# The first 30 microseconds and the last 8 of a decoder trunk: turning the input ahead of all weights, splitting the first weight in two halves, and a shorter final norm

## The chip, the cores and the metric

One Trainium2 chip, one of its cores. The metric is the device time of one execution in microseconds, the median of the runs shown; less is better.

## The reference, cut to what matters

```python
def rmsnorm(x, g):
    y = x * lax.rsqrt(jnp.mean(x * x, axis=-1, keepdims=True) + EPS)
    return y * g

def swiglu(h, w_gate, w_up, w_down):
    return (jax.nn.silu(h @ w_gate) * (h @ w_up)) @ w_down

for i in range(2):                       # x: 512 tokens x 1024
    x = x + 0.5 * swiglu(rmsnorm(x, ffn1_norm[i]), ffn1_w_gate[i], ffn1_w_up[i], ffn1_w_down[i])
    x = x + mixer[i](rmsnorm(x, mix_norm[i]))      # 0: gated linear attention, 1: stick-breaking attention
    x = x + 0.5 * swiglu(rmsnorm(x, ffn2_norm[i]), ffn2_w_gate[i], ffn2_w_up[i], ffn2_w_down[i])
return rmsnorm(x, final_norm)
```

All is float32; the feed-forward width is 2816.

## The kernel before, in words

The residual x is kept turned, as eight tiles `xs[k]` of 128 features x 512 tokens. Every product is made of three TensorE products in float32r (`mm3`, and `prod` in `seven`): each operand is cut into a high part (a cast on ACT, ScalarE) and a low part (a subtraction on DVE, VectorE), and high x high, low x high and high x low are summed. So each weight that arrives costs a cast on ACT (`wh`, L124) and a subtraction on DVE (`wl`, L126).

Weights pass through a queue, `feed`. An `Entry` is a piece of weight with its product; `feed.start()` cuts the weights of the next entries, issues their loads on SP's queue some entries ahead, and returns a generator whose steps are the products. `feat` makes one column block: 128 features x 512 tokens, 8 steps over the 1024 inputs, 24 TensorE products, in `ps_f`. The first two column blocks of the first feed-forward layer have weights of their own of 128 columns (`lead`, four loads of 512 KB: gate, up, gate, up), the next ones 256 columns. From the third 256 columns on, `seven` makes seven products of half size from sums of the weight and of the input (Strassen's form with 7 in place of 8), in two entries: `body_1` and `body_2`, in `ps_w`, `ps_q`, `ps_z`.

A layer starts before its norm is known: gains are multiplied into x ahead, the products run on that, and the norm's factor R is multiplied in when a product is taken out of its bank (`t`, L645 and L652). R comes from the row sums of squares (`stats_a`, with `rstd`: scale and add, square root on ACT, reciprocal on DVE, one Newton step, `r`), and from four products `ps_R` that spread r over the partitions (`stats_b`, which builds the diagonal tiles `dg` and copies `R` out of the bank, L405). `two_halves` starts two entries and runs them in turns, with `stats_a` in between. After the first six column blocks, the input is used with its norm already in (`scaled`: `xn`; cut into `nh`, `nl`), and `seven` also needs sums of it (`ts`, cut into `th`, `tl`).

The start of the program (L1228 to L1280): the gains are loaded into one tile `gl` by four loads on ACT's queue, turned by one TensorE product and copied to `gT`. x is loaded in eight tiles of 128 tokens x 512 features, four of the first half of the features, then the first gate weight, then the other four, then the three other first weights. Each `ps_x` bank takes four turned blocks; from it ACT makes the scaled high part (`xh`, L1260), DVE the low part (`xl`, L1261), and one of both the copy `xs[k]` (L1269, L1271). The squares of the untouched tiles of x (`junk`, L1278) run on ACT, with the row sums as a by-product.

Each engine runs its own instructions in the order in which the built program has them. A scheduler makes this order from the program text, by priorities and by what is ready; `tc.issue_after(ins)` sets an instruction behind another in it. Memory that is used again is waited for.

The last layer (`last`): the down product is made token by token block (`back_tok`), for each of four token blocks two halves of the features. `last` adds the residual on DVE, takes squares on ACT with their sum, and after the second half computes r for the block (`rstd` with n=1), scales both halves by r and the final gain (`fin`), and writes both out.

## Time and profile before

| | |
|---|---|
| Median of 3 runs | 1874.41 us (1874.35 to 1876.14) |
| Profiled execution | 1874.33 us, span from first to last instruction 1872.2 us |
| TensorE (PE) busy | 1847.3 us, 99% of the span |
| VectorE (DVE) busy | 1412.0 us, 75% |
| ScalarE (ACT) busy | 1012.5 us, 54% |
| Granted TensorE clock, mean | 0.998 of full speed |
| DMA, mean | 96 GB/s; 158 in the first fortieth of the span |

A row of the timeline has the start in us, the duration of one (or of so many, xN), the engine, the line of the source, the operation, what it writes and reads (buffer numbers left out), and in brackets how long the engine was idle just before and what ended that. PE is TensorE's product, PEld its weight load. A row of the list of waits has the engine and tile that waited, on what, then us in total, times, and the longest. A row of the table by stretches has the length, then for each engine busy us and instructions, the granted clock, the DMA engines' busy share, and GB/s. An engine's operations overlap a little: durations are longer than the distance from start to start.

### The profile page before, as it was taken

The numbers are of one execution on the slowest core, as the hardware profiler recorded it, in microseconds if no ns is written. First come the engines' busy times: TensorE is split into PE (matmuls) and PEld (weight loads), VectorE is DVE, ScalarE is ACT, GpSimd is POOL, SyncE is SP. The second block draws the span as 40 slices with busy tenths as digits, with TensorE's granted clock in tenths as the row PEclk, the third lists the DMA queues.
The fourth block names the chain that finished last, engine by engine and source line by source line (L and its number), as shares of the span: only waits on it lengthen the run. The fifth ranks groups of instructions, "written<-read, shape, count | busy, mean of one in ns | idle before, by whom it ended". The sixth has DMA issues, their size and how long they took to land.

```text
span 1872.2 us, 29140 instructions
## 1 busy us (share of the span) xinstructions
PE 1847.3 (99%) x11933; PEld 1650.8 (88%) x11933; DVE 1412.0 (75%) x2177; ACT 1012.5 (54%) x1714; POOL 7.3 (0%) x17
## 2 busy tenths in 40 slices
PE   8999999999999999999999999999999999999998
PEld 6899999789888899999888999998888788999997
DVE  7977776775767987777788777676878769777775
ACT  6544545444555554454555545445878755554454
POOL 0000000100000000000000000000000000000000
PEclk9999999999999999999999999999999999999999
DMA  5433333212123233342233333233221223333321
GB/s 158 130 107 110 105 113 103 87 48 66 61 75 113 79 102 102 107 129 80 79 113 116 111 102 113 79 92 101 68 68 57 68 90 113 102 102 102 119 85 68
DMA packets 177513, 179.04 MB, mean 96 GB/s; under 512 B 4034, under 2 KB 167924, under 8 KB 177380
## 3 DMA queue, kind: packets, MB, share of 16 engines
q1 hardware_dynamic: 176768, 176.18, 30.0%
q8 instruction: 93, 1.52, 0.3%
q0 software_dynamic: 512, 0.99, 0.2%
q14 instruction: 40, 0.33, 0.1%
q10 hardware_dynamic: 100, 0.03, 0.0%
HBM read 175.11 MB, written 2.10 MB: 95 GB/s over the span
## 4 chain that ended last, share of the span: by engine, by line
PE 88%; DVE 9%; ACT 1%; issue 1%; DMA 0%; SPq 0%; DVEq 0%; ACTq 0%
PE ps_d L64 25%; PE ps_w L523 20%; PE ps_f L64 11%; PE ps_q L523 10%; PE ps_z L523 5%; PE ps_t L64 5%; PE ps_b L64 4%; DVE wl L126 2%; PE ps_S L64 1%; PE ps_z L1058 1%; PE ps_bt L64 1%; DVE ts L615 1%; DVE xn L599 1%; DVE nl L606 1%; PE ps_oT L1120 1%; PE ps_T L1105 1%
## 5 line engine op out<-in xcount | busy, mean ns | idle before, releaser
L126 DVE TENSOR_TENSOR wl<-raw,wh 128x1024 fp32r<-128x1024 f32 x244 | 259.9, 1066 | 96.6 <-ACT wh L124 61.5
L124 ACT CAST wh<-raw 128x1024 fp32r<-128x1024 f32 x244 | 224.7, 923 | 131.2 <-PE ps_f L64 44.4
L64 PE MATMUL ps_d<-hh,wl 128*128 128x512 f32 x672 | 262.4, 390 | 0.0
L64 PE MATMUL ps_d<-hh,wh 128*128 128x512 f32 x672 | 262.3, 390 | 0.0
L64 PE MATMUL ps_d<-hl,wh 128*128 128x512 f32 x672 | 261.6, 389 | 0.0
L523 PE MATMUL ps_w<-th,wl 128*128 128x256 f32 x864 | 239.1, 277 | 5.0 <-DVE wl L126 5.0
L523 PE MATMUL ps_w<-tl,wh 128*128 128x256 f32 x864 | 239.0, 277 | 0.9 <-DVE tl L606 0.9
L523 PE MATMUL ps_w<-th,wh 128*128 128x256 f32 x864 | 239.2, 277 | 0.2
L307 DVE SCALAR_TENSOR_TENSOR x<-ps_d,x 128x512 f32<-128x512 f32 x184 | 124.9, 689 | 115.9 <-PE ps_d L64 115.6
L126 DVE TENSOR_TENSOR wl<-s,wh 128x1024 fp32r<-128x1024 f32 x144 | 176.1, 1223 | 40.7 <-PE ps_z L523 19.3
L124 ACT CAST wh<-s 128x1024 fp32r<-128x1024 f32 x144 | 151.2, 1050 | 93.2 <-PE ps_q L523 30.0
L124 ACT CAST wh<-rawd 128x1024 fp32r<-128x1024 f32 x84 | 88.4, 1053 | 201.7 <-issue 98.9
L64 PE MATMUL ps_f<-xh,wh 128*128 128x512 f32 x448 | 182.1, 407 | 1.6 <-DVE q L721 1.5
L64 PE MATMUL ps_f<-xl,wh 128*128 128x512 f32 x448 | 175.5, 392 | 0.0
L64 PE MATMUL ps_f<-xh,wl 128*128 128x512 f32 x448 | 175.0, 391 | 0.0
L523 PEld LDWEIGHTS ps_w<-th,wl 128*128 128x128 f32 x864 | 162.3, 188 | 5.8 <-DVE wl L126 5.8
L523 PEld LDWEIGHTS ps_w<-tl,wh 128*128 128x128 f32 x864 | 162.2, 188 | 1.1 <-DVE tl L606 1.1
L523 PEld LDWEIGHTS ps_w<-th,wh 128*128 128x128 f32 x864 | 162.2, 188 | 1.0 <-ACT wh L124 1.0
L64 PEld LDWEIGHTS ps_d<-hl,wh 128*128 128x128 f32 x672 | 126.2, 188 | 26.7
L64 PEld LDWEIGHTS ps_d<-hh,wh 128*128 128x128 f32 x672 | 126.2, 188 | 24.5
L64 PEld LDWEIGHTS ps_d<-hh,wl 128*128 128x128 f32 x672 | 126.2, 188 | 23.8
L126 DVE TENSOR_TENSOR wl<-rawd,wh 128x1024 fp32r<-128x1024 f32 x84 | 102.9, 1225 | 53.6 <-ACT wh L124 40.1
(248 smaller groups left out, 4434.4 us busy)
## 6 DMA issues: line engine op xcount, KB each, us to landing
raw<-in_ffn_w_gate_dram SPq DMA_DIRECT2D x43, 1024.0 KB, 5.3
raw<-in_ffn_w_up_dram SPq DMA_DIRECT2D x43, 1024.0 KB, 5.4
rawd<-in_ffn_w_down_dram SPq DMA_DIRECT2D x84, 512.0 KB, 3.5
raw<-in_gla_w_in_dram SPq DMA_DIRECT2D x12, 1024.0 KB, 5.5
raw<-in_sb_w_in_dram SPq DMA_DIRECT2D x16, 512.0 KB, 3.8
raw<-in_gla_w_out_dram SPq DMA_DIRECT2D x4, 1024.0 KB, 5.0
raw<-in_sb_w_in_dram SPq DMA_DIRECT2D x4, 1024.0 KB, 5.3
raw<-in_sb_w_out_dram SPq DMA_DIRECT2D x4, 1024.0 KB, 5.0
```

Source lines behind the costliest of these rows:

```text
L64: st["pe"] = nc.tensor.matmul(ps, l, r, start=first, stop=last).ins
L124: st["cut"] = nc.scalar.copy(h, r).ins
L126: nc.vector.tensor_tensor(out=l, in0=r, in1=h.bitcast(F32), op=ALU.subtract)
L307: nc.vector.scalar_tensor_tensor(out=xs[k], in0=ps, scalar=0.5, in1=xs[k], op0=ALU.mult, op1=ALU.add)
L523: st["pe"] = nc.tensor.matmul(o, l_, r_, start=first and j + n == 0, stop=j == 3 and n == 2, skip_group_check=True).ins
L599: nc.vector.scalar_tensor_tensor(out=t, in0=xs[k], scalar=g, in1=st["R"], op0=ALU.mult, op1=ALU.mult)
L606: nc.vector.tensor_tensor(out=l, in0=t, in1=h.bitcast(F32), op=ALU.subtract)
L615: nc.vector.tensor_tensor(out=o, in0=p, in1=q, op=ALU.subtract)
L1058: nc.tensor.matmul(o_, l_, r_, start=first, stop=last, skip_group_check=True)
L1105: nc.tensor.transpose(ps[:, c0 : c0 + P], ys[yb][:, yc + j * P : yc + (j + 1) * P], ident)
L1120: nc.tensor.matmul(po[e * 64 : e * 64 + 64, j * P : T], self.v[j][:, c : c + 64], self.wt[p, e][bk][:, c0 : c0 + n], start=j == 0, stop=j ...
```

## The change

- x is loaded whole ahead of all weights; the first gate weight comes behind it in two loads of four of its eight k-blocks each (`parts`), and is cut in two halves too.
- The gains are split over two tiles, so that those of the first norm need one load only; the rest is turned later.
- x is turned tile by tile (four blocks per tile into four banks at once) instead of bank by bank; three more banks follow for the second half, and the eighth later.
- The order of scalings, copies and cuts on ACT and DVE is set by hand (`behind`); six of the eight squares stand behind the cut of the third weight. The constraint that held the cuts behind the gains goes.
- The first column block is started by hand in the start of the program; the first `two_halves` then starts one entry instead of two.
- In `rstd` the sum isn't divided by D: D x EPS is added, and the square root of D goes into the constants of the Newton step. With n=1, two of its multiplications become one, and the sum of the two halves' squares goes into the first addition.
- In `last` the scaled first half is written to a tile of its own (`xf`) instead of over x.

```diff
@@ Chunk.load @@
-                nc.sync.dma_start(self.t, self.src)
+                for c in range(self.parts):
+                    c = slice(c * self.n // self.parts, (c + 1) * self.n // self.parts)
+                    nc.sync.dma_start(self.t[:, c], self.src[:, c])
@@ Entry.split @@
-                    st["cut"] = nc.scalar.copy(h, r).ins
-                    with tc.issue_after(st["gains"]):
-                        nc.vector.tensor_tensor(out=l, in0=r, in1=h.bitcast(F32), op=ALU.subtract)
+                    self.cut = []
+                    for c in range(parts):
+                        c = slice(c * n // parts, (c + 1) * n // parts)
+                        st["cut"] = (
+                            nc.scalar.copy(h[:, c], r[:, c]).ins,
+                            nc.vector.tensor_tensor(
+                                out=l[:, c], in0=r[:, c], in1=h[:, c].bitcast(F32), op=ALU.subtract
+                            ).ins,
+                        )
+                        self.cut.append(st["cut"])
@@ rstd @@
-    def rstd(sums, n):
+    def rstd(sums, n, more=None):
...
-        nc.vector.tensor_scalar(out=v, in0=sums, scalar1=1.0 / D, scalar2=EPS, op0=ALU.mult, op1=ALU.add)
+        nc.vector.tensor_scalar(
+            out=v, in0=sums, scalar1=0.0 if more is None else more, scalar2=D * EPS, op0=ALU.add, op1=ALU.add
+        )
...
-        nc.vector.tensor_tensor(out=q, in0=y, in1=y, op=ALU.mult)
-        nc.vector.tensor_tensor(out=q, in0=q, in1=v, op=ALU.mult)
-        nc.vector.tensor_scalar(out=q, in0=q, scalar1=-0.5, scalar2=1.5, op0=ALU.mult, op1=ALU.add)
+        if n == 1:
+            nc.vector.scalar_tensor_tensor(out=q, in0=y, scalar=v, in1=y, op0=ALU.mult, op1=ALU.mult)
+        else:
+            nc.vector.tensor_tensor(out=q, in0=y, in1=y, op=ALU.mult)
+            nc.vector.tensor_tensor(out=q, in0=q, in1=v, op=ALU.mult)
+        c = float(D) ** 0.5
+        nc.vector.tensor_scalar(out=q, in0=q, scalar1=-0.5 * c, scalar2=1.5 * c, op0=ALU.mult, op1=ALU.add)
@@ two_halves @@
-    def two_halves(between=None):
+    def two_halves(between=None, n=2):
...
-        g = [feed.start(), feed.start()]
+        g = [feed.start() for _ in range(n)]
@@ FFN.run @@
-                two_halves(stats_a)
+                two_halves(stats_a, 2 - (feed.pos == 1))
@@ last @@
         if dh == 0:
-            nc.vector.tensor_tensor(out=x, in0=x, in1=fin[:, 0:T], op=ALU.mult)
+            st["xf"] = st["tp"].tile([P, T], F32, tag="s", bufs=4, name="xf")
+            nc.vector.tensor_tensor(out=st["xf"], in0=x, in1=fin[:, 0:T], op=ALU.mult)
             return
-        s = st["sq"][:, 2 * i : 2 * i + 1]
-        nc.vector.tensor_tensor(out=s, in0=s, in1=sq, op=ALU.add)
-        r = rstd(s, 1)
+        r = rstd(sq, 1, st["sq"][:, 2 * i : 2 * i + 1])
...
-        nc.scalar.activation(xt[i, 0], xt[i, 0], AF.Copy, scale=r)
-        nc.sync.dma_start(rows[:, 0:T], xt[i, 0])
+        nc.scalar.activation(st["xf"], st["xf"], AF.Copy, scale=r)
+        nc.sync.dma_start(rows[:, 0:T], st["xf"])
```

The start of the program is written anew. Its order after the change:

```python
for hf in range(2):
    for i in range(NT):
        x0[i, hf] = ip.tile([P, T], F32, name=f"x0_{i}_{hf}")
        nc.sync.dma_start(x0[i, hf], a["x"][0, i * P : (i + 1) * P, hf * T : (hf + 1) * T])
for c in lead:
    c.pool, c.parts = ip, 2 if c is lead[0] else 1
    c.load()
...
squares(0, (0, 1))
pst = [psum("ps_x") for _ in range(4)]
for i in range(NT):
    if i == 2:
        ...                                     # gains of the first norm: turn, copy
    for k in range(4):
        turn(k, pst[k], i)
done = [scale(k, pst[k]) for k in range(4)]     # xh on ACT, xl on DVE
kept = [keep(k, pst[k]) for k in range(2)]      # xs[k]: even k on ACT, odd k on DVE
pst += [psum("ps_x") for _ in range(3)]
with tc.issue_after(st["pe"]):
    for i in range(NT):
        for k in range(4, 7):
            turn(k, pst[k], i)
with behind([kept[0], kept[1]]):
    feed.q[0].split(parts=2)
pst.append(psum("ps_x"))
...                                             # turn k = 7
with behind(feed.q[0].cut[0]):
    done += [scale(k, pst[k]) for k in range(4, 8)]
    kept += [keep(k, pst[k]) for k in range(2, 4)]
with tc.issue_after(st["pe"]):
    body = feed.q[0].body(feed.q[0].W)
    next(body)                                  # first half of the first column block
with behind(done[7]):
    feed.q[1].split()
    with behind(st["cut"]):
        kept += [keep(k, pst[k]) for k in range(4, 8)]
for _ in body:
    pass
with behind(kept[6:]):
    feed.start()
...                                             # the other gains: turn, copy
with behind(st["cut"]):
    squares(0, (2, 3))
    squares(1, range(NT))
```

More of the change, by code (lines that the diff above doesn't have):

```diff
@@ L79, in __init__ @@
             self.few = False
+            self.parts = 1
         def load(self):
@@ L105, in view, with split @@
             return self.views
-        def split(self):
+        def split(self, parts=1):
             if self.W is None:
@@ L1183, in to_tokens @@
     def to_tokens(tp):
+        st["tp"] = tp
         fin = st["fin"] = tp.tile([P, D], F32, tag="s", bufs=4, name="fin")
@@ L1228, in decoder, with gains @@
     with tc.tile_pool(name="ip", bufs=1) as ip:
-        gl = ip.tile([P, P], F32, name="gl")
-        nc.vector.memset(gl, 0.0)
-        row = 0
-        for nm in ("ffn1_norm", "mix_norm", "ffn2_norm"):
-            nc.scalar.dma_start(gl[row : row + 16], a[nm].rearrange("l (k p) -> (l k) p", p=P))
-            row += 16
-        nc.scalar.dma_start(gl[row : row + 2], a["gla_o_norm"].rearrange("l (k p) -> (l k) p", p=P))
+        gls = [ip.tile([P, P], F32, name=f"gl{n}") for n in range(2)]
+        for gl in gls:
+            nc.vector.memset(gl, 0.0)
+        def gains(n, names):
+            row = n * 16
+            for nm in names:
+                r = a[nm].rearrange("l (k p) -> (l k) p", p=P)
+                nc.scalar.dma_start(gls[n][row : row + r.shape[0]], r)
+                row += r.shape[0]
+        gains(0, ("ffn1_norm",))
+        gains(1, ("mix_norm", "ffn2_norm", "gla_o_norm"))
         x0 = {}
-        st["ss"] = None
-        sums = [ip.tile([P, NT], F32, name=f"sums{hf}") for hf in range(2)]
-        lead = phases[0].lead
         for hf in range(2):
@@ L1243, in decoder @@
                 nc.sync.dma_start(x0[i, hf], a["x"][0, i * P : (i + 1) * P, hf * T : (hf + 1) * T])
-            for c in lead[:1] if hf == 0 else lead[1:]:
-                c.pool = ip
-                c.load()
-        ps = psum("ps_g")
-        nc.tensor.transpose(ps[:, 0:P], gl, ident)
-        st["gains"] = nc.vector.tensor_copy(gT[:, 0:50], ps[:, 0:50]).ins
-        st["nh"], st["nl"], pst = [], [], []
-        for hf in range(2):
-            for k in range(hf * 4, hf * 4 + 4):
-                ps = psum("ps_x")
-                for i in range(NT):
-                    nc.tensor.transpose(
-                        ps[:, i * P : (i + 1) * P], x0[i, hf][:, (k % 4) * P : (k % 4 + 1) * P], ident
-                    )
-                h = np_.tile([P, T], F32R, tag="xh", name="xh")
-                l = np_.tile([P, T], F32R, tag="xl", name="xl")
-                nc.scalar.activation(h, ps, AF.Copy, scale=gT[:, k : k + 1])
-                nc.vector.scalar_tensor_tensor(
-                    out=l, in0=ps, scalar=gT[:, k : k + 1], in1=h.bitcast(F32), op0=ALU.mult, op1=ALU.subtract
-                )
-                st["nh"].append(h)
-                st["nl"].append(l)
-                pst.append(ps)
-            for k in range(hf * 4, hf * 4 + 4):
-                if k % 2:
-                    nc.vector.tensor_copy(xs[k], pst[k])
-                else:
-                    nc.scalar.copy(xs[k], pst[k])
@@ L1272, in decoder @@
-        for e in feed.q[:2]:
-            e.split()
-        for hf in range(2):
-            for i in range(NT):
-                junk = ip.tile([P, T], F32, tag="j", bufs=2, name="junk")
-                with tc.issue_after(st["cut"]) if hf * NT + i >= 6 else ExitStack():
-                    nc.scalar.activation(junk, x0[i, hf], AF.Square, accum_out=sums[hf][:, i : i + 1])
+        lead = phases[0].lead
+        for c in lead:
+            c.pool, c.parts = ip, 2 if c is lead[0] else 1
+            c.load()
@@ new lines, in decoder, with squares, behind @@
+        st["ss"] = None
+        sums = [ip.tile([P, NT], F32, name=f"sums{hf}") for hf in range(2)]
+        st["nh"], st["nl"] = [], []
+        new_norm()
+        def squares(hf, tiles):
+            for i in tiles:
+                junk = ip.tile([P, T], F32, tag="j", bufs=2, name="junk")
+                nc.scalar.activation(junk, x0[i, hf], AF.Square, accum_out=sums[hf][:, i : i + 1])
+        def behind(ins):
+            es = ExitStack()
+            for c in ins:
+                es.enter_context(tc.issue_after(c))
+            return es
@@ new lines, in turn, with scale @@
+        def turn(k, ps, i):
+            x = x0[i, k // 4]
+            t = nc.tensor.transpose(ps[:, i * P : (i + 1) * P], x[:, (k % 4) * P : (k % 4 + 1) * P], ident)
+            st["pe"] = t.ins
+        def scale(k, ps):
+            h = np_.tile([P, T], F32R, tag="xh", name="xh")
+            l = np_.tile([P, T], F32R, tag="xl", name="xl")
+            c = nc.scalar.activation(h, ps, AF.Copy, scale=gT[:, k : k + 1]).ins
+            d = nc.vector.scalar_tensor_tensor(
+                out=l, in0=ps, scalar=gT[:, k : k + 1], in1=h.bitcast(F32), op0=ALU.mult, op1=ALU.subtract
+            ).ins
+            st["nh"].append(h)
+            st["nl"].append(l)
+            return c, d
@@ new lines, in keep @@
+        def keep(k, ps):
+            if k % 2:
+                return nc.vector.tensor_copy(xs[k], ps).ins
+            return nc.scalar.copy(xs[k], ps).ins
+        squares(0, (0, 1))
+        pst = [psum("ps_x") for _ in range(4)]
+        for i in range(NT):
+            if i == 2:
+                psg = psum("ps_g")
+                nc.tensor.transpose(psg[:, 0:P], gls[0], ident)
+                nc.vector.tensor_copy(gT[:, 0:16], psg[:, 0:16])
+            for k in range(4):
+                turn(k, pst[k], i)
@@ new lines, in decoder @@
+        done = [scale(k, pst[k]) for k in range(4)]
+        kept = [keep(k, pst[k]) for k in range(2)]
+        pst += [psum("ps_x") for _ in range(3)]
+        with tc.issue_after(st["pe"]):
+            for i in range(NT):
+                for k in range(4, 7):
[4 more added lines that the diff above has]
+        with tc.issue_after(st["pe"]):
+            for i in range(NT):
+                turn(7, pst[7], i)
@@ new lines, in decoder @@
+        with behind(feed.q[0].cut[0]):
+            done += [scale(k, pst[k]) for k in range(4, 8)]
+            kept += [keep(k, pst[k]) for k in range(2, 4)]
+        with tc.issue_after(st["pe"]):
+            body = feed.q[0].body(feed.q[0].W)
[5 more added lines that the diff above has]
+        for _ in body:
+            pass
+        with behind(kept[6:]):
+            feed.start()
@@ L1279, in decoder @@
+        ps = psum("ps_g")
+        with tc.issue_after(st["pe"]):
+            nc.tensor.transpose(ps[:, 0:P], gls[1], ident)
+        nc.vector.tensor_copy(gT[:, 16:50], ps[:, 16:50])
+        with behind(st["cut"]):
+            squares(0, (2, 3))
+            squares(1, range(NT))
         st["sums"] = sp.tile([P, NT], F32, tag="rq", bufs=2, name="sums")
```

## The prediction

> **What bounds the kernel now.** I read the page's chain first, then the list of waits of TensorE (whole span, then its first 80 us), then busy time by stretches of 5 us, and last the timeline of the first 70 us and of the last 8.

> ```profile
> PE 88%; DVE 9%; ACT 1%; issue 1%; DMA 0%; SPq 0%; DVEq 0%; ACTq 0%
> PE ps_g L1248 <- DMA gl<-in_ffn_norm_dram: 5.8, 1, 5.8
> PE ps_w L523 <- DVE wl L126: 1.4, 1, 1.4
> core 0: us, PE busy (x) PEld busy (x) DVE busy (x) ACT busy (x) POOL busy (x), PEclk, DMA share, GB/s
> 0.00:5.00 5.00, 0.00 (x0) 0.00 (x0) 0.22 (x2) 1.96 (x4) 0.70 (x6) 1.00 0.54 174
> 5.00:10.00 5.00, 3.98 (x17) 3.35 (x17) 0.23 (x2) 3.09 (x8) 0.00 (x0) 1.00 0.91 269
> 10.00:15.00 5.00, 3.65 (x18) 2.99 (x19) 3.90 (x6) 4.49 (x10) 0.00 (x0) 0.81 1.16 326
> 30.00:35.00 5.00, 5.00 (x24) 4.14 (x23) 5.00 (x10) 3.44 (x5) 0.00 (x0) 1.00 0.01 3
> 60.00:65.00 5.00, 5.00 (x44) 4.92 (x43) 5.00 (x9) 2.00 (x6) 0.00 (x0) 1.00 0.00 0
> 65.00:70.00 5.00, 3.58 (x28) 3.19 (x27) 5.00 (x7) 3.76 (x7) 0.00 (x0) 1.00 0.70 210
> ```

> TensorE carries 88% of the chain; only its wait for the first gains (5.8 us, hidden by the loads of x) and one of 1.4 us for VectorE (DVE) stand out in the first 80 us. But DVE's 9% matters here: from 30 to 70 us it is busy all of every stretch. The 1.4 us wait lies at the end of this full stretch. So two clocks run through the start: TensorE, and DVE's unbroken queue from the moment when R (the row norm, spread over the partitions) exists. Whichever is later sets everything behind 70 us, where TensorE doesn't wait up to 200 us and the built order of TensorE is the same before and after.

> ```profile
> 6.76 2.63 PEld L1255 LDWEIGHTS ps_x<-ident,x 128*128 128x128 f32 x13 [0.26 <-DMA x<-in_x_dram]
> 12.34 2.35 PE L1255 MATMUL ps_x<-ident,x 128*128 128x128 f32 x13 [0.41 <-DMA x<-in_x_dram]
> 14.34 0.78 PE L64 MATMUL ps_f<-xh,wh 128*128 128x512 f32 x1
> 16.80 0.39 PE L64 MATMUL ps_f<-xh,wh 128*128 128x512 f32 x1
> 18.62 0.39 PE L64 MATMUL ps_f<-xl,wh 128*128 128x512 f32 x1
> 26.03 0.16 DVE L388 TENSOR_TENSOR r<-ry,rq 128x4 f32<-128x4 f32 x1
> 26.77 1.09 PE L401 MATMUL ps_R<-dg,gT 128*128 128x128 f32 x8
> 28.51 1.22 DVE L126 TENSOR_TENSOR wl<-raw,wh 128x1024 fp32r<-128x1024 f32 x1
> 29.64 0.69 DVE L645 TENSOR_TENSOR t<-ps_f,R 128x512 f32<-128x512 f32 x1
> 66.02 0.38 PE L523 MATMUL ps_w<-th,wh 128*128 128x256 f32 x1
> 66.50 1.23 DVE L126 TENSOR_TENSOR wl<-s,wh 128x1024 fp32r<-128x1024 f32 x1
> 67.78 0.38 PE L523 MATMUL ps_w<-th,wl 128*128 128x256 f32 x1 [1.37 <-DVE wl L126]
> 69.18 0.28 PE L523 MATMUL ps_q<-nh,wh 128*128 128x256 f32 x1
> 69.37 1.23 DVE L126 TENSOR_TENSOR wl<-raw,wh 128x1024 fp32r<-128x1024 f32 x1
> ```

> Landmarks: the fourth tile of x is there by 6.76, the last at 12.34; products begin at 14.34 and run at (18.62-16.80)/8 = 0.2275 us; r is computed at 26.03, and I call tR the time at which DVE first multiplies by R, 29.64. The first product of body_2 then waits for DVE until 67.78, and the next (ps_q) begins at 69.18, which is tR + 39.54. TensorE alone would have been 1.4 us earlier.

> **The change at the front: TensorE starts sooner.** All eight tiles of x now pass before the weights on SP's queue. Two bounds for the second half of the first gate weight (2.1 + 0.52 = 2.62 MB lie up to its end): by the stretches, 0.87 + 1.345 MB have moved by 10.0, and the other 0.41 MB take 1.24 us at 326 GB/s, so 11.2; and in the trace the transfer with the same 2.62 MB up to its end is the last tile of x, 12.34. I take 12.34, the same bytes in the same queue with like transfers behind it, and keep 11.2 for the range. The first half, 0.26 MB ahead at 326 GB/s, lands 0.8 earlier, 11.5. The transposes, gains (now from one load) and the first four scalings are done by then: from 7.4 (fourth tile at 6.76, its turn behind the third's four, 0.2 each) four scalings of 0.61 and one copy of 0.6 (rows below) give 10.4. Products begin near 12.3, 2.0 us earlier than 14.34. Keeping copies (L1269, L1271) behind other work, the second memset and the second turn of gains (0.2 us each) fall into idle time of DVE and cost nothing; without that cover they would add their 0.2.

> **The change to R: it comes later.** The squares of six tiles, which ran in ACT's gaps while it waited for loads, now stand in ACT's order behind three weight casts, and the fourth cast and the table load stand behind the squares. ACT's order in the built program from the second half cast on: four scalings, x2, the up cast, x4, x6, a gate cast, six squares, an up cast, table load, square root.

> ```profile
> 13.57 2.43 ACT L1260 ACTIVATE xh<-ps_x,gT 128x512 fp32r<-128x512 f32 x4
> 17.47 0.64 ACT L1271 COPY x<-ps_x 128x512 f32<-128x512 f32 x1
> 17.93 1.12 ACT L124 CAST wh<-raw 128x1024 fp32r<-128x1024 f32 x1
> 19.97 0.71 ACT L1278 ACTIVATE junk<-x 128x512 f32<-128x512 f32 x1
> 20.60 3.01 ACT L124 CAST wh<-raw 128x1024 fp32r<-128x1024 f32 x3
> 23.62 1.28 ACT L381 ACT_TABLE_LOAD   x1
> 24.92 0.21 ACT L381 ACTIVATE ry<-rv 128x4 f32<-128x4 f32 x1
> 44.70 2.66 ACT L605 CAST th<-ts 128x512 fp32r<-128x512 f32 x4 [1.05 <-PE ps_f L64]
> ```

> Sum: land 12.34 + half cast 0.65 (a quarter of the th row) + scalings 2.43 + three copies 1.8 (0.46 each, if the next one starts as early as at 17.93: 0.45 less, for the range) + three casts 3.01 + six squares at 0.63 (19.97 to 20.60) 3.8 + table 1.30 (23.62 to 24.92) = 25.33 for the square root, 24.92 before: nearly the same, because one cast fewer stands ahead of it and the added idle eats that. But behind it DVE's order has changed. Before: reciprocal, five short ones, R. After, in the built program:

> ```
> Reciprocal ry, wl (first 256-column gate), rq, rq, wl (first 256-column up), rq, r4, dg x4, R, t
> ```

> Both wl wait for ACT casts that only follow the square root. So: square root 0.25, cast 1.05, semaphore 0.05, wl 1.13 (28.51 to 29.64), two short ones 0.40 (0.2 apart), wl 1.13, one short 0.20, r; that is r at 25.33 + 4.21 = 29.54; from r to the next DVE operation behind R is 28.51 - 26.03 = 2.48, so tR = 32.0 against 29.64: 2.4 later (1.3 if the weight lands at 11.2). Queued behind the two wl are r, dg and R, and TensorE's own queue: ps_R stands 13 products into the third column (the start of one entry instead of two, two_halves with n=1). TensorE gets there at 12.3 + 61 x 0.2275 + 1.1 for the slow first products (16.80 - 14.34 for six of them, less 6 x 0.2275) = 27.3 and ps_R can't run before 29.54 + 0.74 = 30.3. The 2.0 us won, and more, is waited away there.

> From tR DVE's work is the same as before up to ps_q's last need, 69.37 - 29.64 = 39.73 us, but one 0.6 us operation (the last tl) has moved behind wl and the next weight, and body_2's first product needs it as its last operand. ps_q begins at tR + 39.73 + 0.1 (write end) + 0.1 (a cast now ahead of another on ACT) + 0.1 = tR + 40.0, before tR + 39.5. Shift at ps_q: 2.4 + 0.5 = +2.9 us (+1.8 with the early landing). TensorE by itself would be there sooner: from ps_R's end, 31.1, 131 products of 0.2275 and five groups of 1.4 (67.78 to 69.18) make 67.9, against 72.0. It hides nothing of the shift and waits 4 us more on the way, 1.1 of them inside body_2's first product, for the moved tl.

> **The final norm.** Two short DVE operations go from the path behind the last product.

> ```profile
> 1864.51 0.69 DVE L1201 SCALAR_TENSOR_TENSOR x<-ps_bt,x 128x512 f32<-128x512 f32 x1 [0.20 <-PE ps_bt L64]
> 1866.05 0.16 DVE L1210 TENSOR_TENSOR gT<-gT 128x1 f32<-128x1 f32 x1 [0.85 <-ACT ps_bt L1204]
> 1866.24 0.15 DVE L379 TENSOR_SCALAR rv<-gT 128x1 f32<-128x1 f32 x1
> 1866.86 0.16 DVE L384 TENSOR_TENSOR rq<-ry 128x1 f32<-128x1 f32 x1
> 1867.06 0.16 DVE L385 TENSOR_TENSOR rq<-rq,rv 128x1 f32<-128x1 f32 x1
> ```

> L1210 goes into the scalar of rv (0.19, start to start), the two rq become one (0.20): -0.4 us. The merged forms aren't in the trace; all short ones take 0.15 to 0.16, the big two-operand form takes no more than the one-operand one, so they may give back at most 0.1. xf in a tile of its own frees DVE from ACT's square for the first three token tiles, where nothing waits; the two output transfers stay last, in the same order.

> **Sum.** +2.9 - 0.4 = +2.5 us on the profiled execution's 1874.33 (span 1872.2 plus 2.1 around it): 1876.8; the median of the runs shown is 0.08 above it, so 1876.9. That is 0.13% slower; within 0.2% (3.75 us, about what a measurement of this kernel can tell from no change) it counts as the same.

> **Rivals.** First, the end at the other side of no change: TensorE's clock. The trace has a stretch at half clock:

> ```profile
> 13.00:13.50 0.50, 0.50 (x5) 0.50 (x4) 0.50 (x2) 0.42 (x1) 0.00 (x0) 0.60 1.22 292
> 16.50:17.00 0.50, 0.50 (x3) 0.40 (x3) 0.50 (x2) 0.50 (x2) 0.00 (x0) 0.99 1.14 330
> ```

> It lasts from 13 to 16.5 after a TensorE that was idle more than busy; a stretch of 3.4 us at half speed loses 1.7 us. The wait of 1.4 us at 67.78 left the clock at 1.00. After the change TensorE waits 3.0 us at ps_R (27.3 to 30.3) and up to 3 in one piece before body_2. If the clock falls at the second, TensorE restarts slowly with nothing left to hide it: 1876.9 + 1.7 = 1878.6, slower. If at ps_R, the th casts (which wait for TensorE's sixth product, the th row above) now stand in ACT's order ahead of a cast that DVE needs, and DVE slips by the same 1.7. It decides from a gap somewhere above 1.4 us. Both new gaps lie above that, and the idle start, which ended at half clock, was longer: chance 0.2. [...]

> Second, faster: DVE isn't the later clock, because its queue catches up (it has 1.8 us less to do between tR and body_2: one wl of 1.13 and one tl of 0.6 are elsewhere). Then TensorE's own start counts: -2.0, the wait of 1.4 goes, -0.4 at the end: 1874.4 - 3.8 = 1870.6. For it: the wait in the trace is only 1.4, and with R no later than before it would shrink. Against it: R hangs on the two wl, and DVE shows no idle to catch up in. Chance 0.1.

> Third, the split buys what it can: the second half lands at 11.2 and the shift is 1.8: 1875.8, still the same; chance 0.1. Or it buys nothing, because both halves land together behind interleaved transfers, 1 us later than 12.34: 1877.9, at the edge; chance 0.1.

> **Numbers.** Forecast and its bounds 0.5, early landing 0.1, late landing 0.1, clock 0.2, faster 0.1. The range reaches from the early landing without my 0.5 us at ps_q and the copies' 0.45 (1874.85), and 0.45 further towards the faster case, which can hold in part (1874.4), to the clock rival and the 0.4 not won (1879.0); the faster case is left out. Faster over 0.2% 0.1, same 0.63, slower 0.27 (the clock 0.2, half of the late landing, 0.02 of the forecast's upper end).

> **What would show it.** Right: products begin near 12.3; the square root near 25.3 with wl between reciprocal and r; ps_R near 30.3 after a wait of TensorE for dg of 2 to 3 us; t (L645 before) near 32; a wait of TensorE for wl of 2 to 3 us in body_2; two operations fewer behind the last product. Wrong: t before 30; no wait at ps_R; idle DVE between 32 and 68; half clock beyond 17 us.

## The result and the profile after

The changed kernel takes 1878.29 us (median of 17 runs, 1876.07 to 1882.35), the kernel before 1874.35 on the same chip (17 runs, 1873.57 to 1876.72): ratio 1.0021, interval 1.0014 to 1.0029, so 3.9 us slower. The forecast was 1876.9, the range 1874.4 to 1879.0. Two profiles of the changed kernel follow; the second is a run repeated for this (e9).

First profile (1879.36 us), the waits of TensorE in the first 100 us, below the line for the loads of x (5.5 us in two waits):

```profile
PE ps_R L418 <- DVE dg L414: 2.2, 1, 2.2
PE ps_w L540 <- ACT wh L131: 1.0, 1, 1.0
PE ps_w L540 <- DVE wl L132: 0.9, 1, 0.9
PE ps_q L540 <- DVE wl L132: 0.4, 1, 0.4
PE ps_w L540 <- DVE tl L623: 0.3, 1, 0.3
```

Where there was one wait of 1.4 us for VectorE behind the first products, there is one of 2.2 at ps_R and four, 2.6 us together, around body_2, all for VectorE or ScalarE. The timeline at the landmarks of the prediction (start, length, engine, line):

```profile
13.34 0.62 ACT L131 CAST wh<-raw 128x512 fp32r<-128x512 f32 x1 [0.28 <-DMA raw<-in_ffn_w_gate_dram]
13.11 0.68 PE L64 MATMUL ps_f<-xh,wh 128*128 128x512 f32 x1
25.54 0.20 ACT L394 ACTIVATE ry<-rv 128x4 f32<-128x4 f32 x1
26.72 1.23 DVE L132 TENSOR_TENSOR wl<-raw,wh 128x1024 fp32r<-128x1024 f32 x1 [0.76 <-ACT wh L131]
28.13 1.22 DVE L132 TENSOR_TENSOR wl<-raw,wh 128x1024 fp32r<-128x1024 f32 x1
29.47 0.16 DVE L405 TENSOR_TENSOR r<-ry,rq 128x4 f32<-128x4 f32 x1
30.08 1.64 PE L418 MATMUL ps_R<-dg,gT 128*128 128x128 f32 x8 [2.18 <-DVE dg L414]
32.48 0.69 DVE L662 TENSOR_TENSOR t<-ps_f,R 128x512 f32<-128x512 f32 x1
73.71 0.42 PE L540 MATMUL ps_q<-nh,wh 128*128 128x256 f32 x1
77.05 0.40 PE L64 MATMUL ps_d<-hh,wh 128*128 128x512 f32 x1
```

Products begin 1.2 us sooner than before (13.11 against 14.34), R is first used 2.84 later (32.48 against 29.64), ps_q begins 4.53 later (73.71 against 69.18). Between root (25.54) and r (29.47) stand the two low cuts. ps_d, the first product behind body_2, began at 72.00 before; it is 5.05 later, and the shift stays near that to the end (1879.36 - 1874.33 = 5.03). The same kernel, second profile (1877.57 us):

```profile
24.81 0.21 ACT L394 ACTIVATE ry<-rv 128x4 f32<-128x4 f32 x1
29.35 1.16 PE L418 MATMUL ps_R<-dg,gT 128*128 128x128 f32 x8 [2.20 <-DVE dg L414]
31.27 0.69 DVE L662 TENSOR_TENSOR t<-ps_f,R 128x512 f32<-128x512 f32 x1
71.51 0.41 PE L540 MATMUL ps_q<-nh,wh 128*128 128x256 f32 x1
74.80 0.40 PE L64 MATMUL ps_d<-hh,wh 128*128 128x512 f32 x1
```

The same wait of 2.2 us at ps_R, yet four ps_R products take 1.16 instead of 1.64 us, and ps_d is 2.80 late, not 5.05 (3.24 at the end; where the other 0.4 us are lost wasn't looked for). Of the 2.25 us between the two, 0.73 are an earlier landing of the first weight (the root at 24.81, not 25.54); the rest is the clock. Busy time by stretches (from:to, length, busy time and instructions of PE, PEld, DVE, ACT, POOL, granted clock, DMA share, GB/s), first profile:

```profile
27.18:30.59 3.41, 1.23 (x8) 0.77 (x7) 3.23 (x10) 1.74 (x2) 0.00 (x0) 1.00 0.03 9
30.59:34.00 3.41, 3.41 (x12) 2.90 (x12) 2.24 (x5) 0.63 (x1) 0.00 (x0) 0.50 0.00 0
68.13:71.55 3.42, 1.50 (x10) 1.11 (x10) 3.42 (x5) 2.92 (x4) 0.00 (x0) 1.00 0.51 119
71.55:74.96 3.41, 3.14 (x15) 2.84 (x14) 3.41 (x5) 1.71 (x3) 0.00 (x0) 0.50 1.01 332
```

Second profile:

```profile
24.90:28.31 3.41, 2.25 (x10) 1.52 (x9) 2.46 (x5) 3.29 (x4) 0.00 (x0) 1.00 0.21 68
28.31:31.72 3.41, 2.37 (x14) 2.13 (x15) 2.57 (x9) 0.00 (x0) 0.00 (x0) 1.00 0.00 0
65.85:69.26 3.41, 1.63 (x12) 1.23 (x11) 3.41 (x5) 2.83 (x4) 0.00 (x0) 1.00 0.46 112
69.26:72.67 3.41, 3.20 (x16) 2.91 (x15) 3.41 (x5) 1.80 (x3) 0.00 (x0) 0.50 1.04 336
```

The third number from the right is the granted clock. In the first profile it is halved from 30.59 to 34.00 and from 71.55 to 74.96: each 3.41 us long, and 40.96 apart, which is 12 times 3.413. In the second it is halved only from 69.26 to 72.67. The rows ahead of the halved ones show TensorE busy for 1.23, 1.50 and 1.63 of 3.41 us. At ps_R in the second profile the same gap of 2.2 us falls across two such stretches (boundaries worked back from 69.26 in steps of 3.413), busy 2.25 and 2.37 us, and the clock stays full.

### The profile page after: what moved, and what is told of

Same layout as the page of the kernel before. It is cut to its first block, busy times and chain, and to the rows that moved or that the text cites. A ratio compares the mean times of both kernels' runs of the same rounds, so it can differ in the third digit from the quotient of the medians.

```text
span 1877.4 us, 29143 instructions
## 1 busy us (share of the span) xinstructions
PE 1851.1 (99%) x11934; PEld 1653.4 (88%) x11934; DVE 1411.8 (75%) x2172; ACT 1012.0 (54%) x1715; POOL 7.3 (0%) x17
## 4 chain that ended last, share of the span: by engine, by line
PE 89%; DVE 8%; ACT 1%; DMA 1%; issue 1%; SPq 0%; DVEq 0%; ACTq 0%
PE ps_d L64 25%; PE ps_w L540 20%; PE ps_f L64 13%; PE ps_q L540 10%; PE ps_z L540 5%; PE ps_t L64 5%; PE ps_b L64 4%; DVE wl L132 2%; PE ps_S L64 1%; PE ps_z L1076 1%; PE ps_bt L64 1%; PE ps_oT L1138 1%; PE ps_T L1123 1%; DVE ts L632 1%; PE ps_o L64 1%; DVE xn L616 1%
## 5 line engine op out<-in xcount | busy, mean ns | idle before, releaser
L132 DVE TENSOR_TENSOR wl<-raw,wh 128x512 fp32r<-128x512 f32 (+1 forms) x245 | 259.5, 1059 | 95.3 <-ACT wh L131 61.6
L131 ACT CAST wh<-raw 128x512 fp32r<-128x512 f32 (+1 forms) x245 | 225.0, 919 | 131.0 <-PE ps_f L64 45.0
L64 PE MATMUL ps_d<-hh,wl 128*128 128x512 f32 x672 | 262.3, 390 | 0.0
L64 PE MATMUL ps_d<-hh,wh 128*128 128x512 f32 x672 | 262.3, 390 | 0.0
L64 PE MATMUL ps_d<-hl,wh 128*128 128x512 f32 x672 | 261.6, 389 | 0.0
L64 PE MATMUL ps_f<-xh,wh 128*128 128x512 f32 x448 | 182.3, 407 | 1.5 <-DVE q L739 1.5
L64 PE MATMUL ps_f<-xl,wh 128*128 128x512 f32 x448 | 175.7, 392 | 0.0
L64 PE MATMUL ps_f<-xh,wl 128*128 128x512 f32 x448 | 175.3, 391 | 0.0
L64 PEld LDWEIGHTS ps_d<-hl,wh 128*128 128x128 f32 x672 | 126.2, 188 | 26.7
L64 PEld LDWEIGHTS ps_d<-hh,wh 128*128 128x128 f32 x672 | 126.2, 188 | 24.5
L64 PEld LDWEIGHTS ps_d<-hh,wl 128*128 128x128 f32 x672 | 126.2, 188 | 23.8
```

Source lines behind the costliest of these rows:

```text
L64: st["pe"] = nc.tensor.matmul(ps, l, r, start=first, stop=last).ins
L131: nc.scalar.copy(h[:, c], r[:, c]).ins,
L132: nc.vector.tensor_tensor(out=l[:, c], in0=r[:, c], in1=h[:, c].bitcast(F32), op=ALU.subtract).ins,
```

## The experiments

The theory: (A) R is late because of the order of squares, casts and low cuts, and from the first multiplication by R (t) VectorE works unbroken, so that body_2 is as late as t; the halved clock comes on top, in the gaps that this makes. The rival (B): gap and clock are the whole loss. Ratios are against the kernel before, from runs on the same chip; they come from all of these runs, so the quotient of two medians can differ from them by up to 0.0004. Code is shortened.

**e1: low cuts behind R.**

```
+    def cut_low(l, r, h, e):
+        late = e in feed.q[4:6]
+        with tc.issue_after(st["Rins"]) if late else ExitStack():      # Rins: the copy of R
+            return nc.vector.tensor_tensor(out=l, in0=r, in1=h.bitcast(F32), op=ALU.subtract).ins
```

> The changed kernel with one thing different: VectorE's low cuts (wl) of the weights of the third column's two halves, which stand between the reciprocal and r4, are put behind the copy of R. Their number stays. Theory A (R comes late by the order on VectorE and ScalarE, and from the first multiplication by R on VectorE works without a gap, so that it sets when body_2 may go on): r4 is ready about 2.4 us sooner (27.0 instead of 29.5), TensorE finds the last dg ready when it reaches ps_R at 27.5 and does not wait (2.18 us before), no half clock follows there; but both low cuts, 2 x 1.22 us, must now be done between R and the first multiplication, so VectorE starts on those at about 31.5 to 32.0 instead of 32.5, and body_2 waits about 2 us more than in the changed kernel. Time about 1877.3 on the scale where before is 1874.4 (ratio 1.0015). Rival B (the gap at ps_R and the half clock behind it are themselves the price): gap and clock go, 2.2 + 0.9 us, and nothing comes in their place: 1875.2 (1.0004). Rival C (the loss lies in neither): unchanged at 1878.3 (1.0021).

Measured: 1877.93 us, ratio 1.0015 (1.0006 to 1.0023). Its timeline:

```profile
28.91 1.22 DVE L98 TENSOR_TENSOR wl<-raw,wh 128x1024 fp32r<-128x1024 f32 x1
30.05 0.68 DVE L665 TENSOR_TENSOR t<-ps_f,R 128x512 f32<-128x512 f32 x1
```

Busy time by stretches:

```profile
67.28:70.69 3.41, 1.80 (x11) 1.41 (x11) 3.41 (x5) 2.54 (x5) 0.00 (x0) 1.00 0.81 272
70.69:74.10 3.41, 2.92 (x13) 2.92 (x14) 3.41 (x5) 1.29 (x2) 0.00 (x0) 0.50 0.64 189
```

TensorE's wait at ps_R shrank from 2.2 to 0.3 us, and the time hardly moved. That is A's number, and B's 1.0004 lies outside the interval. C's 1.0021, no change, lies inside it, so the time alone doesn't separate A from C; and the clock fell after all, in body_2 (the second row above). One detail was wrong: only one low cut stood between R and t (28.91), so t came at 30.05, not 31.5 to 32. The other came later in the same queue: from t to ps_q (71.56) it was 41.51 us, not 40. The work was moved, not saved.

**e2: R behind 72 products.** two_halves starts two entries again (n=2) for the first layer, and the third column's evacuation is deferred.

> The changed kernel with the fourth column's entry started beside the third as in the kernel before, so that ps_R stands behind 72 products instead of 60; VectorE's and ScalarE's order ahead of R stays. TensorE reaches ps_R at about 30.2 instead of 27.5, when the last dg (30.6) is nearly ready, so the gap there shrinks from 2.2 to about 0.4 us and VectorE's first multiplication by R comes at about 32.1 instead of 32.5. Theory A (VectorE's queue behind R sets the end of body_2): the wait moves into body_2 in whole, about 4 us there, ps_q at the first multiplication plus 40.0; time 1877.0 (ratio 1.0014), lower than the changed kernel only by what the half clock at 30.5 to 34 cost. Rival B (the half clock behind the gap at ps_R is most of the loss): 1875.2 to 1875.6 (1.0004 to 1.0006). Rival C: the clock falls in the longer gap of body_2 instead, 1878 (1.002).

Measured: 1878.35 us, ratio 1.0020 (1.0010 to 1.0030). Its profiled run took 1881.99; timeline:

```profile
32.88 0.68 DVE L663 TENSOR_TENSOR t<-ps_f,R 128x512 f32<-128x512 f32 x1
```

Busy time by stretches:

```profile
67.49:70.90 3.41, 1.80 (x11) 1.40 (x11) 3.41 (x5) 2.84 (x4) 0.00 (x0) 1.00 0.67 219
70.90:74.31 3.41, 2.49 (x11) 2.49 (x12) 3.41 (x5) 1.42 (x2) 0.00 (x0) 0.50 0.81 243
74.31:77.73 3.42, 3.42 (x17) 3.34 (x16) 1.60 (x4) 0.17 (x1) 0.00 (x0) 0.50 0.00 0
```

No gap at ps_R and a full clock there, and no gain. B is out; A's 1.0014 and C's 1.002 both lie in the interval, and the trace speaks for C: the gap moved into body_2, where the clock was halved for two stretches. It was halved for a third from 658.00 to 661.41; that begins 587.10 us after the first, 172 times 3.413 to within 0.1 us. The order ahead of R didn't stay as expected: both low cuts of the third column went behind the diagonals, so r was there at 27.39 instead of 29.47. VectorE then waited 1.3 us for ps_R, now behind more products, and t came at 32.88, where I had put 32.1.

**e3: three squares into ScalarE's idle time.**

```
         kept = [keep(k, pst[k]) for k in range(2)]
+        with behind([kept[0]]):
+            squares(0, (2, 3))
+            squares(1, range(1))
```

> The changed kernel with three of the six late squares on ScalarE moved into its idle time at 10.2 to 12.4 us, ahead of the first weight's cut. The square root comes about 1.9 us sooner, at 23.65 instead of 25.54, and one of the two low cuts falls behind dg. Theory A: r4 at about 26.8, TensorE (27.5) waits at most 0.4 us for dg, VectorE's first multiplication by R at about 29.8 instead of 32.5, about where it stood in the kernel before (29.64); ps_q of body_2 at about 69.8; no half clock at ps_R; body_2's wait about 2.5 us, since TensorE starts 1.2 us sooner than before. Time 1874.4 (ratio 1.0000), or 1875.2 (1.0005) if the clock falls in body_2. Rival B (the order of the low cuts alone makes R late): half of that, 1876.3 (1.0010). Rival C (the loss is not in R's lateness): 1878 (1.002).

Measured: 1874.91 us, ratio 1.0000 (0.9991 to 1.0009). Its timeline:

```profile
22.74 0.21 ACT L394 ACTIVATE ry<-rv 128x4 f32<-128x4 f32 x1
28.63 0.69 DVE L662 TENSOR_TENSOR t<-ps_f,R 128x512 f32<-128x512 f32 x1
68.73 0.28 PE L540 MATMUL ps_q<-nh,wh 128*128 128x256 f32 x1
71.56 0.40 PE L64 MATMUL ps_d<-hh,wh 128*128 128x512 f32 x1
```

The loss is gone with three squares moved: the root came 2.8 us sooner, 1.8 by the squares and 1.0 because the second half of the weight was cut 1.0 sooner in this run; t at 28.63, ps_q 40.10 and ps_d 42.93 behind it. A's time was met; t came even 1.2 us below A's number, 1.0 of it by that weight. Against the second profile, with nearly the same landing (cut at 12.60, here at 12.4), the root is 2.07 us and t 2.64 us sooner. The waits in body_2 are 2.1 us, in pieces, and the clock stays full there (1.00 from 63.79 to 70.61).

**e5: the final norm alone**, put into the kernel before.

> The kernel before with only the changed final norm (rstd, last and to_tokens of the changed kernel). From the two traces the tail from the end of part at L1210/L1220 to the last store is 4.08 instead of 4.30 us: time lower by 0.22 us, 1874.2 (ratio 0.9999). The prediction's term: lower by 0.40 us. Rival: the pointer operands make the short operations as slow as the ones that they replace, no difference. None of these can be told apart by the time alone; the tail in the trace tells it.

Measured: 1874.08 us, ratio 0.9997 (0.9988 to 1.0006): not to be told from none by the time. Its timeline:

```profile
1864.33 0.69 DVE L1209 SCALAR_TENSOR_TENSOR x<-ps_bt,x 128x512 f32<-128x512 f32 x1 [0.50 <-PE ps_bt L64]
1866.56 0.22 DVE L388 SCALAR_TENSOR_TENSOR rq<-ry,rv 128x1 f32<-128x1 f32 x1
1868.42 0.38 SPq L1220 DMA_DIRECT2D out_dram<-x  x1
```

From the last evacuation to the last store 4.09 us, against 1868.81 - 1864.51 = 4.30 before: 0.21 won. The two merged forms, which take a scalar from memory, last 0.21 and 0.22 instead of 0.15 and 0.16, and what stands behind them starts 0.05 later each.

**e6: filling the gaps.** Nine products whose results nobody reads ahead of ps_R, and 8, 8 and 4 small ones ahead of body_2's first three products.

```
+        for _ in range(9):      # in stats_b, ahead of ps_R
+            nc.tensor.matmul(ps, st["h"][0][:, 0:P], st["h"][1], start=True, stop=True, ...)
+                        for _ in range(fill[n] if j == 0 else 0):      # body_2: fill = (8, 8, 4)
+                            nc.tensor.matmul(v["w"][:, H:T], st["h"][0][:, 0:P], st["h"][1][:, 0:H], ...)
```

> The changed kernel with extra products whose results are never read, on TensorE alone, where it would stand idle: nine of 128x512 shortly ahead of ps_R and 8, 8 and 4 of 128x256 ahead of the first three products of body_2. The order on VectorE and ScalarE stays, so R is as late as in the changed kernel. In the profiled runs so far the clock fell for 3.4 us (once for 6.8) after stretches of 3.4 us in which TensorE was busy for about half the time or less. Theory A (two separate causes: R's lateness, and the halved clock in the gaps that it makes): no halved clock at 27 to 36 and at 66 to 78; first multiplication by R at about 32.2, ps_q at that plus 40.0, about 72.3 where the changed kernel had 73.7, ps_d at ps_q plus 2.85; what is left over the kernel before is R's lateness alone: time 1876.9 (ratio 1.0010), with a smaller spread of the runs than the changed kernel's 1876.1 to 1882.4. Rival B (the clock is the whole loss): ratio 1.0000. Rival C (the clock costs nothing, VectorE sets all): 1878.3, ratio 1.0021.

The small ones write into the bank in which body_2 adds up, and change its sums; only the time is read. Measured: 1877.36 us (1876.39 to 1878.64), ratio 1.0014 (1.0005 to 1.0023). Its timeline:

```profile
29.64 1.16 PE L420 MATMUL ps_R<-dg,gT 128*128 128x128 f32 x8 [2.22 <-DVE dg L416]
31.55 0.69 DVE L670 TENSOR_TENSOR t<-ps_f,R 128x512 f32<-128x512 f32 x1
67.84 1.12 PE L543 MATMUL ps_w<-nh 128*128 128x256 f32 x8
67.81 0.68 DVE L631 TENSOR_TENSOR tl<-ts,th 128x512 fp32r<-128x512 f32 x1
68.41 1.21 DVE L132 TENSOR_TENSOR wl<-s,wh 128x1024 fp32r<-128x1024 f32 x1
71.64 0.28 PE L547 MATMUL ps_q<-nh,wh 128*128 128x256 f32 x1
74.47 0.39 PE L64 MATMUL ps_d<-hh,wh 128*128 128x512 f32 x1
```

Half of the experiment missed its aim: the scheduler placed the nine products earlier, took nine others out from in front of ps_R for them, and left the gap there at 2.22 us; in this run it didn't halve the clock. In body_2 the gaps were filled: the list of waits has none of TensorE there, and behind the first products no halved clock is left up to the end of the last product.

It isn't the changed kernel's lateness by itself, though t + 40.09 for ps_q looks like the 40.0 that I expected. The built order of VectorE changed too: the last tl stands ahead of the low cut wl again, 36.26 and 36.86 us behind t, as in the kernel before (wl at 66.50 - 29.64 = 36.86). In the changed kernel's first profile it follows behind them, 40.12 us behind t:

```profile
72.60 0.68 DVE L623 TENSOR_TENSOR tl<-ts,th 128x512 fp32r<-128x512 f32 x1
```

With VectorE as in the kernel before, ps_q would have come at t + 39.54 = 71.09 (an estimate from its rows); the 20 added products held TensorE 0.55 us longer, about as long as the moved tl does in e3. That the two are alike is luck. B still is out for body_2: without a halved clock there, the interval lies above 1.0000, and 0.55 us is only 0.0003. The spread agrees weakly: of 26 runs of the changed kernel five took over 1881.5 us, of these 11 none over 1878.64, which chance alone would give about once in seven times.

**e7: R ahead of the stream**, a first try at a better version: one square on ScalarE and three on VectorE more before the first cut, the root before the third column's weights, ps_R inside the second column.

> The changed kernel with the sums and the square root put into the start of the program: four squares more in the time before the first weight lands (one on ScalarE, three on VectorE), the root before the weights of the third column, the diagonals and ps_R inside the second column, and the low cuts of the third column behind the root and around dg. Theory A (what counts is when VectorE can start to multiply by R, and how much of its work is done by then): ps_R without a wait of TensorE at about 27; the first multiplication at about 28.7, as in the run with three squares moved (28.63); ps_q of body_2 at about 68.7; with the shorter final norm 1873.5 (ratio 0.9995), or 1874.7 (1.0000) where the clock falls in body_2. Rival B (more squares on VectorE ahead of the first cut delay the first weight's low half and so the first products): start of the products 1 us later, 1874.9 (1.0001).

Measured: 1876.32 us, ratio 1.0014 (1.0005 to 1.0023). Both theories missed. Its timeline:

```profile
29.83 0.69 DVE L665 TENSOR_TENSOR t<-ps_f,R 128x512 f32<-128x512 f32 x1
```

The root still stood behind a cast that waits 1.47 us for TensorE to free a weight tile, VectorE was idle 2.26 us for the root, and t came at 29.83 instead of 28.7. And as in e1 one more low cut stood behind t: ps_q began at 71.06, 41.23 behind it. Something of B came as well: the first product began at 12.75, but the second waited 0.44 us for a low cut that stood behind the squares, and the clock was halved from 11.15 to 17.98.

**e8: the first weight in one load** (parts 1 for 2).

> The changed kernel with the first weight in one load and one cut, as in the kernel before. In the changed kernel's trace the first half was cut at 12.44 and the second at 13.34, products began at 13.11. In one piece the cut begins when the whole weight has landed, 13.3, and takes about 1.07: products begin at about 13.8 to 14.2, 0.7 to 1.1 us later, and so do the cuts behind it; but two cuts of 0.62 and two of 0.69 become one of 1.07 and one of 1.22, so the square root comes only about 0.5 us later. Theory A (R's lateness sets the time): ps_q 0.3 to 0.6 later, time 1878.7 (ratio 1.0024). Rival B (the halves are the cause of the loss): 1876 (1.0008). Rival C (no effect, since TensorE waits for VectorE anyway): 1878.3 (1.0021).

Measured: 1880.63 us (5 runs), ratio 1.0032 (1.0019 to 1.0045). The cut began at 13.42, products at 14.51, the root at 26.04, 0.5 later as expected. B, that the halves are the loss, is out; A's 1.0024 and C's 1.0021 both lie in the interval. By the ratios the halves are worth 1.5 to 2.1 us (against e9 and the first comparison), but the intervals overlap, and the trace, taken in the slowest of the five runs, doesn't show it at R: one low cut went behind the diagonals, so t came at 32.23, between the 31.27 and 32.48 of the changed kernel, and ps_q at 73.16, between its 71.51 and 73.71. What this run has more of is halved clock: 10.24 us from 10.59, 6.83 from 72.03 and 3.41 from 659.12. Whether the halves gain anything beyond that stays open.

**e9: the changed kernel again.**

> The changed kernel once more, unchanged, for a second profile of it. In the profiles so far every stretch of halved clock lasted 3.4 us or a multiple, and its beginnings within one run lay whole multiples of 3.41 us apart, while from run to run they lay elsewhere against the program. Theory A (the clock is judged over successive stretches of 3.41 us whose phase against the program differs from run to run): R's lateness is the same in this profile (first multiplication by R between 31.5 and 32.5), the halved clock is placed otherwise or missing at ps_R or in body_2, and the profiled times differ by it: each missing stretch takes 0.5 to 1.5 us off the first profile's 1879.4. Median 1878.3 (ratio 1.0021). Rival B (the gap itself sets the clock off, always): the same two stretches as in the first profile, at 30.6 and at 71.5 after the same shift as the products.

Measured: 1877.86 us (9 runs), ratio 1.0024 (1.0014 to 1.0034). Its profile stands above: halved once instead of twice, and t at 31.27, a little below A's 31.5. Rival B is out.

**e10 and e12: R early, low cuts behind it; e11: the root ahead of two copies.** In e10 all eight squares, the root and the diagonals are done in the start of the program; in e11 two copies also follow the root:

```
+        with behind(kept):
+            squares(0, (2, 3)); squares(1, (0,)); squares_v(1, (1, 2))     # squares_v: on VectorE
...                                                     # behind the second weight's cut:
+                squares(1, (3,))
+                st["sums"] = ...                       # sums[0] + sums[1]
+                st["r4"] = rstd(st["sums"], NT)
+                with behind([st["rv"], st["sqrt"]]):   # e11; in e10 copies 4 and 6 ahead of rstd
+                    kept += [keep(k, pst[k]) for k in (4, 6, 5, 7)]
...
+            dgs = diag()                               # low cuts of feed.q[2:6] behind the last dg
+        two_halves(lambda: stats_b(None, dgs), 1)      # ps_R inside the second column
```

> The changed kernel with the statistics ahead of all that kept them late in the trace: three squares on ScalarE and two on VectorE before the first weight's cut, the last one behind the second weight's cut, the square root ahead of the casts of the second column's weights, the four diagonals ahead of all low cuts from the third weight on, ps_R inside the second column. Theory A (VectorE works without a gap from the first multiplication by R to body_2, so every us by which that comes sooner with the same cuts done shortens body_2's wait, until TensorE is the later one): square root at about 20, dg done at about 22.3, ps_R without a wait, first multiplication by R at about 26.3 instead of 28.63 in the run with three squares moved; TensorE waits in body_2 under 0.5 us instead of 2.1; ps_d at about 69.5 instead of 71.56; time 1872.6 (ratio 0.9990). Rival B (the earlier root and table load delay the second column's weights, TensorE waits there instead): 1874.4 (1.0000). Rival C (another wait takes over later, so that body_2's gain is given back): 1874.4 as well, with ps_d at 69.5.

> The kernel of e10 with ScalarE's two copies of x (18.1 to 19.2 us there) moved behind the square root. In e10 VectorE stood idle 0.92 us for the root (20.52). The root should come at about 19.5, and all behind it on VectorE 0.9 us sooner: dg done at about 22.2, first multiplication by R at about 26.2 instead of 27.1 (as far as the start of the products is the same). Theory A (body_2's wait is as long as VectorE is late): body_2's wait shrinks from about 2.0 to about 1.1 us, ps_d at about 69.6 against e10's 70.44, time 1872.2 (ratio 0.9989). Rival B (the casts of the second column's weights become the later ones): no change against e10, ratio 0.9993, VectorE waits for ScalarE's casts of the third weight instead.

> The kernel of e10 once more, beside e11 on the same chip. Theory A: ratio between 0.9990 and 0.9996, time 1873.1; its profile differs from e10's by where the halved clock lies, and by the landing of the first weight; with TensorE's gaps in body_2 together under 2.2 us it may or may not have a halved stretch there (plus 0.5 to 1.2 us).

Measured: e10 1873.11 us, ratio 0.9993 (0.9984 to 1.0002); e12 1873.20, 0.9991 (0.9983 to 1.0000); e11 1872.59, 0.9987 (0.9978 to 0.9996), faster than both kernels. The intervals of e10 and e12 reach 1.0000, so these two aren't told from the kernel before by the time; the two traces are alike (t 27.09 and 27.07, ps_d 70.44 and 70.43). e10's timeline:

```profile
27.09 0.68 DVE L669 TENSOR_TENSOR t<-ps_f,R 128x512 f32<-128x512 f32 x1
70.44 0.40 PE L64 MATMUL ps_d<-hh,wh 128*128 128x512 f32 x1
```

e11's timeline:

```profile
25.56 0.68 DVE L669 TENSOR_TENSOR t<-ps_f,R 128x512 f32<-128x512 f32 x1
69.34 0.40 PE L64 MATMUL ps_d<-hh,wh 128*128 128x512 f32 x1
```

t falls by 1.53 us from e10 to e11 (0.6 of it from an earlier first weight), ps_d by 1.10. From e3 to e10 it was 1.54 and 1.12. Each step of R forward moved body_2 forward, as A says, by about 0.7 us for each us. Not every us arrived: TensorE still waits in body_2 for a low cut, 1.2 us in e10 and 1.0 in e11 by the list of waits, where I expected under 0.5 in e10 already, and t stands at 27.09 in e10 instead of 26.3. Behind body_2 some is given back: ps_d is 2.66 us sooner in e11 than in the kernel before, the profiled run only 2.05 (1872.28 against 1874.33).

## Why the prediction was right, and where it was off

The time lay in the range, 1.4 us above the forecast. By the prediction's own line, 0.2% for "the same", it is on the edge: +0.21%, interval 0.14 to 0.29.

The mechanism was the forecast's, and the first rival came on top. e3 has the low cuts of body_2 and the last tl as far behind t as the second profile (36.26 and 39.14 us), and a full clock there: t to ps_q 40.10, t to ps_d 42.93, where the kernel before has 39.54 and 42.36. With these, the 5.05 us at ps_d in the first profile are 2.36 for R (t would be at 32.00 without the 0.48 that the clock cost between r and t), 0.57 for the moved tl, and 2.12 for the clock (0.48, and 44.57 - 42.93 behind t). The 2.80 in the second profile are 1.63, 0.57 and 0.60. At full clock ps_q would have been late by 32.00 + 40.10 - 69.18 = 2.92 and by 2.19, against +2.9 in the forecast. So halved clock is about two fifths of the loss in one profile and a fifth in the other; for the median, 3.9 us, the share isn't known.

- Start of the products, 12.3: measured 13.11 and 12.36. The second half was cut from 13.34 and from 12.60 on; the forecast had 12.34. In e1, e2, e10 and e12 it was 13.18 to 13.26, so the late landing, given 0.1, was common, though not for its reason: the halves were cut 0.9 us apart.
- ScalarE's sum, 12.99 us from that landing to the root: 12.20 and 12.21 measured. The term that was too large is the chain of single lengths: back to back, a cast, the scalings and three copies took 4.23 us in the second profile (to the start of the next cast, the second weight's cast left out) where I had 4.88. Starts, not lengths, had to be added.
- Root to r, 4.21: measured 3.93 both times, with both wl where the built order had them. r to t, 2.48: 2.53 at full clock, 3.01 at half.
- t at 32.0: 31.27 and 32.48. At full clock the first profile would have just the 32.0 of the forecast, by luck: 1.0 for the late landing against 0.79 and 0.28 for the shorter sums.
- TensorE's wait at ps_R, 3.0 us: 2.2, for dg, as named. From t to ps_q, 40.0: 40.10 in e3, 40.24 in e9; the moved tl is among the waits of body_2.
- "R's lateness makes the loss": shown by e3 (R early, the loss goes) and e10, e11 (earlier still, down to below the kernel before); e1 (the gap at ps_R goes, the time hardly moves) agrees.
- The final norm, -0.4: -0.21 and -0.22. Failed was the bound that the merged forms give back at most 0.1.
- The clock, given 0.2: it came, in one of two profiles at ps_R and in both in body_2. That it decides "from a gap somewhere above 1.4 us" was the step that failed: the length of the gap alone didn't tell. With a gap of 2.2 us at ps_R the clock halved where TensorE was busy 1.23 us in the 3.41 us ahead (27.18 to 30.59, first profile), and stayed full where the gap lay across two stretches of that length, busy 2.25 and 2.37 us (second profile). Nor was TensorE "idle more than busy" ahead of the halving at 13.10: it was busy 1.86 of 3.41 us (last section). The slip of VectorE that I priced at 1.7 us for a halving at ps_R was 1.47: 0.48 at R, and 0.99 from t to body_2's first low cut (37.25 us in the first profile, 36.26 in the second and in e3), 0.75 of it in one wait for a cast (below).
- The signs: of those for being right, the wait in body_2 came in pieces, 1.3 us for low cuts of weights, 1.0 for a cast and 0.3 for tl, not as 2 to 3 for wl. Of those for being wrong, two came: half clock beyond 17 us, and in the first profile 0.75 us of idle VectorE between 32 and 68. Both belong to the first rival.

First profile, VectorE, timeline:

```profile
42.52 1.29 DVE L623 TENSOR_TENSOR nl<-xn,nh 128x512 fp32r<-128x512 f32 x2 [0.75 <-ACT nh L622]
```

## What to carry to other kernels

Where an engine off the chain works without a gap up to the next wait, what counts is the moment at which its unbroken stretch begins and how much work is left in it (in e1 and e7 one cut more behind t took back most of what t had won: ps_q came 41.51 and 41.23 us behind t, 40.10 in e3). Feeding the main engine sooner only made it wait sooner here: products began 1.2 us earlier, ps_q 4.53 later. Before moving small statistics behind large casts, look at what they then stand behind in their engine's built order, and put what releases the stretch ahead of all that isn't needed yet (e11 against the change: 5.7 us between the medians, 6.4 by the ratios). And price a gap of the matrix engine twice: by its length, and by the halved clock that can follow (2.2 us at ps_R, with 3.41 us at half clock behind it in one profile of two).

## What the runs showed of the hardware

Busy time doesn't separate the two outcomes. Cut in steps of 3.413 us from its halvings, the first profile has the clock kept after 1.87 us (6.70 to 10.11) and 1.91 (375.33 to 378.75), and the kernel before has it kept after 0.46 us at the start of the program (2.86 to 6.27). In e6 it was kept after 1.78 us, at its gap of 2.22 us. A halved clock stayed halved after 2.49 us in e2 and 2.81 in e8, and came back after 2.92 in e1. The kernel before, two rows, and e6, one (its stretches counted back from the halving at 1872.25, behind the last product):

```profile
9.69:13.10 3.41, 1.86 (x11) 1.19 (x11) 2.02 (x3) 2.85 (x8) 0.00 (x0) 1.00 1.11 347
64.30:67.71 3.41, 2.06 (x16) 1.66 (x15) 3.41 (x6) 3.06 (x5) 0.00 (x0) 1.00 0.48 118
25.64:29.05 3.41, 1.78 (x8) 1.13 (x6) 2.71 (x6) 2.84 (x3) 0.00 (x0) 1.00 0.10 30
```

The products of the kernel before begin at half clock, behind the first row; behind the second, with its wait up to 67.78, the clock stayed at 1.00 (67.71 to 71.12). What decides where both outcomes occur was not tried.
